# Attention's projections in a stage of their own, two blocks at once in seven products

## The chip, the cores and the metric

The kernel runs on one core of a Trainium2 chip. The core has a matrix engine (TensorE, PE in the profile, with its weight loads as PEld), VectorE (DVE), ScalarE (ACT), GpSimd (POOL), and SyncE (SP), which here issues most of the DMAs. Each engine works through its own queue in order; semaphores tie the queues together. The metric is the device time of one execution in microseconds; lower is better. PE is given its matrix products in a one-pass float32 format, so a float32 value is kept as two parts, a high and a low one, and a product is made of three matmuls.

## What is computed

A decoder trunk of two layers over 16 learned tokens and 1024 given ones, 1040 in all (L), with width 1024 and 16 heads of 64. Layer 0 is a state-space mixer and a gated feed-forward network, layer 1 attention and another such network. The change touches only what lies between the first network and the second: keys and values are projected from the normalized stream, queries from the same stream with another gain, and a "stick-breaking" attention follows.

```python
kv = _rmsnorm(h, kv_norm) @ w_kv
k_shared, v_shared = ...   # 16 heads of 64 each
q = (_rmsnorm(h, sb_norm[j]) @ sb_w_q[j]).reshape(b, L, SB_HEADS, SB_HEAD_DIM)
o = _stick_breaking_attention(q, k_shared, v_shared).reshape(b, L, SB_WIDTH)
h = h + o @ sb_w_o[j]
...
    logits = jnp.einsum('bthd,bshd->bhts', q[:, t0:t1], k[:, :t1]) * scale
    visible = s_idx < t_idx
    log_keep = jnp.where(visible, jax.nn.log_sigmoid(-logits), 0.0)
    later = lax.cumsum(log_keep, axis=3, reverse=True) - log_keep
    log_w = jnp.where(visible, jax.nn.log_sigmoid(logits) + later, -jnp.inf)
    w = jnp.exp(log_w)
    outs.append(jnp.einsum('bhts,bshd->bthd', w, v[:, :t1]))
```

The kernel writes a weight as a difference of two running products of keep probabilities, so the output of a head is a sum over differences of neighbouring values.

## The kernel before

Its stages follow one another: the mixer with its output projection, then the network's `up` and `down` products, attention, the projection of its output (`o_proj`), and `up` and `down` once more. Tokens lie along the columns and features along the 128 rows.

**The seven-product scheme.** `up` and `down` of layer 0 compute a 2 by 2 block product of matrices with seven products of half the size instead of eight (Strassen's scheme). `forms` and `up_sums` make the sums and differences of operands, and three of the products continue in PSUM banks that already hold others. In `up`, a product of a block is 4 x 3 matmuls of some 260 columns; `up` has 22 blocks on two token halves.

**What lies around attention.** `down` finishes in four column quarters of 260 tokens. Its last operation for a feature tile is the residual add in `accumulate` (line 399). After each of three token tiles (TT: 348, 348 and 344 columns) `to_attention` calls `norm`: it makes the high and low parts `uh`, `ul` of the stream, the square sums and the factor of the norm, and spills the stream to DRAM (`h1_d`).

**Attention.** It goes through eight pairs of heads. For each pair come 18 steps: a chunk i of 116 tokens (9 chunks) against a token tile jj of keys at or before it. In a step, `weigh` multiplies queries and keys of both heads (`lg`, 4 matmuls, line 1413), ACT makes the sigmoid (line 1414), POOL masks the diagonal chunk (`affine_select`, line 1418) and DVE scans the running products, once for each head (line 1422). `turn` transposes the result on PE (`wT`, up to 6, line 1435), and ACT copies it to SBUF (line 1439). When two chunks are complete, `values` multiplies them with the values (`po`, line 1450, in bursts of 12 to 60 matmuls), and ACT adds the value of the chunk's end as a bias (line 1457). The calls of this stage are made in an order written out by hand, and PE, DVE, ACT and POOL run in just that order: `flush(LAG)` with LAG = 2 puts the transposes of a step three steps behind its logits.

**The projections** lie between these steps. `heads` gives each pair a `load` of its weights (scaled on DVE, lines 1303 to 1307, split on ACT and DVE) and `half`, one half of a projection of one kind (k, q or v) for one token tile: 12 matmuls of 348 columns into a bank `pj`. The table `halves` of `attention` says which half falls in which step, most of them for the next pair. The results are scaled by the norm's factor on DVE, then `stack` (queries) and `key` (keys) bring high and low parts into the rows in which the products need them, with DMAs from SBUF to SBUF (lines 1356 to 1358 and 1373); `place` transposes the differences of the values (`pv`, line 1384). In the last pair, from its tenth step on, no projections remain, and the banks that they had go to the logits: four banks for `lg` instead of two.

The transfers of this stage are issued by SP in program order (178 of them), except for the outputs `o_d`, which ACT issues.

## Time and profile before

| what | before |
|---|---|
| median of 3 runs | 2854.01 us (2853.3 to 2854.32) |
| the profiled execution | 2852.52 us, span 2850.8 us, mean granted PE clock 0.997 |
| attention, from the last matmul of down to the first matmul of `o_proj` | 1526.15 to 2046.80 us, 520.65 us |
| one pair of heads | 64.50 us |

The profile lists busy time by engine, and beside it the trace gives groups of instructions by line, windows of time, the chain of work that ended last and the instructions in order. In a row of windows, the busy time of each engine stands with the number of instructions in parentheses, then the granted clock of PE as a share of the full one, the DMA engines' share and GB/s. In a row of groups, `x64 | 26.6, 424 | 17.1` means 64 instructions, 26.6 us busy, 424 ns each in the mean, and 17.1 us of idle time of the engine just before them. A busy time of PE counts each matmul from its start to its modelled end; these overlap, so what a matmul costs is read from the distance between starts.

### The profile page before, as it was taken

Reading aid. Unit: us, or ns where it says so; the run is one execution under the profiler, and the core shown is the slowest. Engines: PE = TensorE matmul, PEld = TensorE weight load, DVE = VectorE, ACT = ScalarE, POOL = GpSimd, SP = SyncE. Lnnn points to the kernel's source line nnn. Section 1 sums busy time; section 2 is a strip of 40 time slices with the busy share of each in tenths; the row PEclk is TensorE's granted clock in tenths of the full one; section 3 lists DMA queues with packets and bytes.
Section 4 is the critical chain, followed back from the end, with each engine's and each line's share of the span. In section 5 each row is a group of like instructions: output and inputs, shape, how many; then the busy total and the mean of one; then the engine's idle time right before and its main releaser. Section 6 shows DMA issues by size and latency. Waiting matters only on the chain.

```text
span 2850.8 us, 54962 instructions
## 1 busy us (share of the span) xinstructions
PE 2808.9 (99%) x21808; PEld 2698.9 (95%) x21808; DVE 2000.2 (70%) x3736; ACT 1551.8 (54%) x3060; POOL 619.2 (22%) x542
## 2 busy tenths in 40 slices
PE   8999999999999999999999999999999999999998
PEld 5999999999999999999999999999998999999888
DVE  5687777776587565658986666666679556557895
ACT  5578676673255555555334555555536555555442
POOL 0000000000005666650000111111002666661000
PEclk9999999999999999999999999999999999999999
DMA  6234333314322222236142222222441222225331
GB/s 178 68 111 118 101 103 96 108 58 165 97 80 75 82 76 81 77 102 205 53 136 82 68 67 62 71 62 55 153 145 55 82 76 81 82 76 185 111 111 60
DMA packets 134128, 274.69 MB, mean 96 GB/s; under 512 B 16464, under 2 KB 68304, under 8 KB 133872
## 3 DMA queue, kind: packets, MB, share of 16 engines
q1 hardware_dynamic: 128560, 260.26, 29.2%
q10 hardware_dynamic: 4048, 6.36, 0.6%
q0 software_dynamic: 1264, 4.57, 0.5%
q8 instruction: 171, 2.80, 0.4%
q14 instruction: 85, 0.70, 0.1%
HBM read 203.02 MB, written 53.21 MB: 90 GB/s over the span
## 4 chain that ended last, share of the span: by engine, by line
PE 87%; DVE 3%; DMA 1%; ACT 1%; issue 0%; ACTq 0%; DVEq 0%; SPq 0%
PE p L165 10%; PE p L167 10%; PE p L166 10%; PE acc L166 8%; PE acc L167 8%; PE acc L165 8%; PE pj L165 7%; PE pj L166 7%; PE pj L167 7%; PE lg L1413 3%; PE po L1450 3%; PE wT L1435 3%; PE y L679 1%; PE S L667 1%; PE y L681 1%; DVE bl L930 1%
## 5 line engine op out<-in xcount | busy, mean ns | idle before, releaser
L165 PE MATMUL pj<-uh,wh 128*128 128x348 f32 (+2 forms) x1536 | 500.7, 326 | 1.1 <-DVE h L399 1.1
L166 PE MATMUL pj<-ul,wh 128*128 128x348 f32 (+2 forms) x1536 | 495.1, 322 | 0.0
L167 PE MATMUL pj<-uh,wl 128*128 128x348 f32 (+2 forms) x1536 | 491.6, 320 | 0.0
L165 PE MATMUL p<-bh,fh 128*128 128x262 f32 (+1 forms) x1408 | 401.2, 286 | 10.4 <-DVE p L1054 4.9
L166 PE MATMUL p<-bl,fh 128*128 128x262 f32 (+1 forms) x1408 | 400.3, 285 | 0.5 <-DVE bl L930 0.2
L167 PE MATMUL p<-bh,fl 128*128 128x262 f32 (+1 forms) x1408 | 398.5, 284 | 0.3 <-DVE fl L985 0.3
L165 PE MATMUL p<-bh,wh 128*128 128x262 f32 (+1 forms) x1056 | 300.6, 285 | 1.0 <-ACT bh L929 1.0
L167 PE MATMUL p<-bh,wl 128*128 128x262 f32 (+1 forms) x1056 | 300.9, 285 | 0.0
L166 PE MATMUL p<-bl,wh 128*128 128x262 f32 (+1 forms) x1056 | 300.2, 284 | 0.6 <-DVE bl L930 0.6
L165 PEld LDWEIGHTS pj<-uh,wh 128*128 128x128 f32 x1536 | 288.5, 188 | 3.4 <-ACT wh L1313 1.3
L166 PEld LDWEIGHTS pj<-ul,wh 128*128 128x128 f32 x1536 | 289.0, 188 | 1.2
L167 PEld LDWEIGHTS pj<-uh,wl 128*128 128x128 f32 x1536 | 288.6, 188 | 0.1
L165 PEld LDWEIGHTS p<-bh,fh 128*128 128x128 f32 x1408 | 267.5, 190 | 12.4 <-DVE p L1054 5.3
L293 DVE SCALAR_TENSOR_TENSOR c<-p,params,c 128x260 f32<-128x260 f32 (+1 forms) x440 | 208.6, 482 | 92.7 <-ACT c L289 90.4
L166 PEld LDWEIGHTS p<-bl,fh 128*128 128x128 f32 x1408 | 267.8, 190 | 1.6 <-DVE bl L930 1.3
L167 PEld LDWEIGHTS p<-bh,fl 128*128 128x128 f32 x1408 | 266.7, 190 | 0.7 <-DVE fl L985 0.5
L985 POOL TENSOR_TENSOR fl<-x,fh 128x1024 fp32r<-128x1024 f32 x80 | 192.3, 2404 | 248.2 <-ACT fh L984 248.2
L1054 DVE TENSOR_TENSOR p<-p,ft 128x262 f32<-128x262 f32 (+1 forms) x176 | 76.5, 436 | 216.0 <-ACT ft L1051 124.0
L166 PE MATMUL acc<-gl,wh 128*128 128x260 f32 (+1 forms) x672 | 211.3, 320 | 0.4 <-DVE gl L1152 0.4
L167 PE MATMUL acc<-gh,wl 128*128 128x260 f32 (+1 forms) x672 | 208.7, 320 | 0.0
L165 PE MATMUL acc<-gh,wh 128*128 128x260 f32 (+1 forms) x672 | 204.0, 319 | 0.0
L165 PEld LDWEIGHTS p<-bh,wh 128*128 128x128 f32 x1056 | 201.1, 190 | 1.5 <-ACT bh L929 1.2
(320 smaller groups left out, 7223.9 us busy)
## 6 DMA issues: line engine op xcount, KB each, us to landing
w<-in_w_up SPq DMA_DIRECT2D x92, 512.0 KB
w<-in_w_down SPq DMA_DIRECT2D x44, 512.0 KB
w<-in_w_in SPq DMA_DIRECT2D x40, 512.0 KB
E<-ea_d SPq DMA_DIRECT2D x32, 464.0 KB
D<-acs_d SPq DMA_DIRECT2D x32, 420.5 KB
g<-c SPq DMA_DIRECT2D x88, 130.0 KB
g<-c SPq DMA_DIRECT2D x88, 128.0 KB
b<-g SPq DMA_DIRECT2D x16, 520.0 KB
```

What stands on the lines that cost most here:

```text
L165: mm(out, wh, uh, start=first, stop=False, skip_group_check=joins)
L166: mm(out, wh, ul, start=False, stop=False, skip_group_check=joins)
L167: mm(out, wl, uh, start=False, stop=last, skip_group_check=joins)
L293: nc.vector.scalar_tensor_tensor(to, ps[:, o + i : o + i + n], wcol(i), out, op0=ALU.mult, op1=ALU.add)
L667: nc.tensor.matmul(ps, bk[:n], xde[:n].rearrange("p h d -> p (h d)"), start=True, stop=True)
L679: nc.tensor.matmul(y, xdt[:n, i, :], dk[:, i, :], start=True, stop=c == 0)
L681: nc.tensor.matmul(y, state[:, i, :], ce[:, i, :], start=False, stop=True)
L985: (self.nc.vector if b < 2 else self.nc.gpsimd).tensor_tensor(lo[:, :n], t, hi[:, :n].bitcast(F32), op=ALU.subtract)
L1054: add = lambda o, x, y: tt(o[:, :N], x[:, :N], y[:, :N], op=ALU.add)
L1413: nc.tensor.matmul(ps[:nt, a, :m], part[:, c0 : c0 + nt], ks[a][:, s0 : s0 + m], start=x == 0, stop=x == 1)
L1435: nc.tensor.transpose(pt[:ns, x * CB : x * CB + nt], kp[a][:nt, x * CB : x * CB + ns], self.ident[:nt, :nt])
L1450: nc.tensor.matmul(po[64 * a : 64 * a + 64, w], v[: CH[c][1], c, 64 * a : 64 * a + 64], wt[a][: CH[c][1], c, :nt], start=x == 0, stop=x == ...
```

## The change

The projections leave attention and become a stage between `down` and attention, `head_rows`. It has 12 blocks (the list `HP`): queries, then values, then keys, each for four groups of two head pairs. Two neighbouring pairs and two neighbouring token quarters form the 2 by 2 scheme, so a block takes seven products of 4 x 3 matmuls with 260 columns for each of two token halves.

- `down` gets `end`: the residual add of its last quarter writes into tiles of its own instead of `h`. `head_entry` takes the place of `to_attention`: it spills the stream and makes the forms (`head_forms`) of the first token half while `down` runs. `norm`, `scaled_project` and the classes' `half`, `key`, `stack` and `place` are gone.
- The stream is not normalized before the products. `factors` reads it again from DRAM, makes the factor of the norm during the first blocks, and `put` multiplies keys and values by it; queries get it in the sigmoid's scale as before.
- `put` writes the results to DRAM: `q_d` (high and low part), `k_d` (four slabs of 64 rows) and `v_d`. `turned` reads the values again, makes the differences, transposes them and writes `vt_d`.
- `heads` has only loads left: keys, values and queries of a pair come from DRAM in the rows that the products need.
- In attention, `LAG` is 3 and `kp` has 8 buffers. `lg2` has two buffers throughout. The bias of the outputs is one add on DVE for two chunks, except where they lie in different token tiles; there ACT adds it as before. SP issues 514 transfers in the two stages, against 178 in the stage before.

```diff
-LAG = 2
+LAG = 3
+HP = [(k, p) for k in "qvk" for p in range(0, PAIRS, 2)]
...
-        self.nc.vector.tensor_tensor(h[f][:, o], h[f][:, o], ps[:, :n], op=ALU.add)
+        self.nc.vector.tensor_tensor(h[f][:, o] if to is None else to, h[f][:, o], ps[:, :n], op=ALU.add)
...
+    def head_forms(self, h, end, t, tiles, pool):
...
+        b12, b22 = ([end[k + x][:, :F] if t else h[k + x][:, c0 + F : c0 + 2 * F] for k in half] for x in (0, KD // 2))
...
+        yield from parts(0, b11, first)
+        yield from parts(1, b21)
+        yield from parts(5, b22, others)
+        yield from parts(2, b22, lambda k: tt(b22[k], b21[k], b22[k], op=ALU.subtract))
+        yield from parts(3, t1)
+        yield from parts(4, b12)
+        yield None
+        yield from parts(6, b22)
...
+        def put(kind, p, j, x):
+            x, c = x[:, :F], slice(F * j, F * j + F)
+            if kind == "q":
+                for i, y in enumerate(split(x)):
+                    nc.sync.dma_start(qd[p, i, :, c], y)
+                return
+            t = self.tmp(kind)[:, :F]
+            tt(t, x, r[:, HALO + F * j : HALO + F * j + F], op=ALU.mult)
+            if kind == "v":
+                nc.sync.dma_start(vd[p, :, c], t)
+                return
+            hi, lo = split(t)
+            for i in range(2):
+                nc.sync.dma_start(kd[p, 3 * i, :, c], hi[64 * i : 64 * i + 64])
+                nc.sync.dma_start(kd[p, 1 + i, :, c], lo[64 * i : 64 * i + 64])
...
+            x = product(0, self.mm("p"))
+            p1 = copy(x)
+            yield
+            y = product(2, self.sm("p"))
+            add(y, y, p1)
+            u2 = copy(y)
+            yield
+            z = product(3, (self.ex if next(turn) else self.lg)("p"))
+            p5 = copy(z)
+            add(z, z, u2)
+            yield
+            put(kind, p, 2 * t, product(1, x, False))
+            yield
+            add(p5, product(4, y, False), p5)
+            put(kind, p + 1, 2 * t + 1, p5)
+            yield
+            put(kind, p, 2 * t + 1, product(5, z, False))
+            yield
+            put(kind, p + 1, 2 * t, product(6, y, False))
...
+            for _ in zip(s, t):
+                for _ in range(4 if n < 4 else 2):
+                    next(chores, None)
...
+            if kind == "v":
+                chores = chain(chores, turned(p), turned(p + 1))
...
-        kp = pool.tile([P, 2, TW], F32, tag="kp", name=self.nm("kp"), bufs=6)
+        kp = pool.tile([P, 2, TW], F32, tag="kp", name=self.nm("kp"), bufs=8)
...
-            nc.scalar.activation(os[p][:, c0 : c0 + nt], po[:, b * CB : b * CB + nt], AF.Identity, bias=ends[:, i : i + 1])
...
+            nc.vector.tensor_tensor(three(os[i0 // 3 * 3][:, c0 : c0 + k * nt], nt), three(po[:, : k * nt], nt),
+                                    ends[:, i0 : i1 + 1].unsqueeze(2).to_broadcast([P, k, nt]), op=ALU.add)
...
+        loads = {(0, 2): ("q", 2), (-1, 9): ("k",), (-1, 10): ("q", 0), (-1, 11): ("v",), (-1, 13): ("q", 1)}
...
-                ps = both(more if p + 1 == PAIRS and n > 8 and n % 2 else self.lp)
+                ps = self.lp.tile([P, 2, 512], F32, tag="lg2", name=self.nm("lg"), bufs=2)
...
-                for own, pair in now.items():
-                    if (own, n) in halves:
-                        late += pair.half(*halves[own, n])
```

PE's queue in the middle of a pair, before the change: transposes `wT`, logits `lg`, and then the first of 12 matmuls of a projection (`pj`, from the stream's parts `uh`, `ul` and the weights' parts `wh`, `wl`).

```order
L1435 MATMUL wT_21715<-ident,kp_21573 116x116 x3
L1435 MATMUL wT_21720<-ident,kp_21573 116x116 x3
L1413 MATMUL lg_21725<-k_21142,qs_21499 116x116 x2
L1413 MATMUL lg_21725<-k_21143,qs_21501 116x116 x2
L165 MATMUL pj_21737<-uh_16937,wh_21458 128x348
L166 MATMUL pj_21737<-ul_16938,wh_21458 128x348
L167 MATMUL pj_21737<-uh_16937,wl_21459 128x348
```

The same queue after the change, in a pair's later steps:

```order
L1573 MATMUL lg_21580<-k_21354,qs_21409 116x348 x2
L1573 MATMUL lg_21580<-k_21355,qs_21412 116x348 x2
L1595 MATMUL wT_21595<-ident,kp_21467 116x116 x3
L1595 MATMUL wT_21600<-ident,kp_21467 116x116 x3
L1573 MATMUL lg_21605<-k_21354,qs_21409 116x348 x2
L1573 MATMUL lg_21605<-k_21355,qs_21412 116x348 x2
L1595 MATMUL wT_21619<-ident,kp_21497 116x116 x3
L1595 MATMUL wT_21624<-ident,kp_21497 116x116 x3
```

Logits and transposes now follow one another with nothing between them, except for the bursts of `po`.

DVE's queue at the end of `down`, before the change: the last residual add (line 399), then the low parts of the first pair's weights, their scaling, and the low part and squares of the last token tile.

```order
L399 TENSOR_TENSOR h_14628<-h_14628,acc_17369 128x260
L1315 TENSOR_TENSOR wl_17457<-w_2276_17450,wh_17456 128x512
L1307 TENSOR_TENSOR w_2281_17462<-w_2281_17462,params 128x512 x2
L270 TENSOR_TENSOR ul_16952<-h_14628,uh_16951 128x344
L237 TENSOR_TENSOR sq_17405<-sq_17405,sq_17425 128x344
```

After the change, from the 22nd row behind the last residual add: low parts of a form (line 1279), scaling of the next block's weights (1313), the first two adds between products of the first block (1468), and further forms (1289).

```order
L1279 TENSOR_TENSOR bl_17478<-ft_17354,bh_17477 128x260
L1313 TENSOR_TENSOR w_2313_17752<-w_2313_17752,params 128x512
L1468 TENSOR_TENSOR p_17455<-p_17455,c_17431 128x260
L1289 TENSOR_TENSOR ft_17291<-ft_17291,ft_17437 128x260
L1313 TENSOR_TENSOR w_2383_18141<-w_2383_18141,params 128x512
L1289 TENSOR_TENSOR ft_17312<-ft_17312,ft_17441 128x260
L1313 TENSOR_TENSOR w_2383_18141<-w_2383_18141,params 128x512
L1289 TENSOR_TENSOR ft_17333<-ft_17333,ft_17445 128x260
L1289 TENSOR_TENSOR ft_17354<-ft_17354,ft_17449 128x260
L1468 TENSOR_TENSOR p_17487<-p_17487,c_17469 128x260
```

The first of these adds is the 28th row behind the last residual add, the second the 35th.

SP's queue in a block of keys after the change, with stores of four half tiles and of turned values:

```order
L1404 DMA k_d<-hi_20444 64x260
L1405 DMA k_d<-lo_20445 64x260
L1404 DMA k_d<-hi_20444 64x260
L1405 DMA k_d<-lo_20445 64x260
L1449 DMA vt_d<-vt_20461 116x2x128
L1449 DMA vt_d<-vt_20464 116x128
```

Before the change SP had no stores to DRAM here besides those of the stream.

More of the change, by code (lines that the diff above doesn't have):

```diff
@@ L1090, in up, with down @@
         return d
-    def down(self, layer, gd, hd, pool, after):
+    def down(self, layer, gd, hd, pool, after, end=None):
         nc, a, F = self.nc, self.a, FNS[layer]
@@ new lines, in head_entry @@
+    def head_entry(self, h, j, res, h1, end, pool):
+        F = FNS[0]
+        if res is None:
+            forms = [{}, {}]
+            res = [self.head_forms(h, end, t, forms[t], pool) for t in range(2)], forms, []
+        works, forms, first = res
+        if j == 0:
+            self.spill_tile(h, h1, 0, 2 * F)
+            for _ in range(6 * KD // 2):
+                next(works[0])
+        elif j == 1:
+            self.spill_tile(h, h1, 2 * F, F)
+            g, v = self.head_raw(0)
+            first += [g, v, *self.head_sums(0, g, v, pool)]
+        else:
+            for k in range(KD):
+                self.nc.sync.dma_start(h1[k, :, 3 * F :], end[k][:, :F])
+            for _ in works[0]:
+                pass
+        return res
@@ new lines, in turned, with block, product, copy @@
+                yield
+        def block(n, t, w):
+            kind, p = HP[n]
+            def product(i, ps, start=True):
+                wh, wl, c0 = w[i]
+                for k in range(KD // 2):
+                    c = slice(c0 + k * P, c0 + k * P + P)
+                    self.mm3(ps[:, :F], wh[:, c], wl[:, c], *forms[t][i][k], start and k == 0, k == KD // 2 - 1, not start)
+                return ps
+            def copy(ps):
+                s = self.ft(pool) if n else self.tmp("c")
+                nc.scalar.activation(s[:, :F], ps[:, :F], AF.Copy)
+                return s
+            add = lambda o, x, y: tt(o[:, :F], x[:, :F], y[:, :F], op=ALU.add)
+            x = product(0, self.mm("p"))
+            p1 = copy(x)
+            yield
+            y = product(2, self.sm("p"))
+            add(y, y, p1)
+            u2 = copy(y)
+            yield
+            z = product(3, (self.ex if next(turn) else self.lg)("p"))
+            p5 = copy(z)
+            add(z, z, u2)
+            yield
+            put(kind, p, 2 * t, product(1, x, False))
+            yield
+            add(p5, product(4, y, False), p5)
+            put(kind, p + 1, 2 * t + 1, p5)
+            yield
+            put(kind, p, 2 * t + 1, product(5, z, False))
+            yield
+            put(kind, p + 1, 2 * t, product(6, y, False))
+            yield
@@ new lines, in head_rows @@
+        turn = cycle((0, 0, 1))
+        rest, chores = works[1], iter(())
+        for n, (kind, p) in enumerate(HP):
+            if n == 0:
+                w = self.head_weights(0, *first, pool)
+            else:
+                g, v = self.head_raw(n)
+                w = self.head_weights(n, g, v, *self.head_sums(n, g, v, pool), pool)
+            s, t = (block(n, t, w) for t in range(2))
+            if n == 0:
+                for _ in s:
+                    for _ in range(5):
+                        next(rest, None)
+                for _ in rest:
+                    pass
+                for _ in t:
+                    pass
+                chores = factors()
+                continue
+            for _ in zip(s, t):
+                for _ in range(4 if n < 4 else 2):
+                    next(chores, None)
+            if n == 3:
+                for _ in chores:
+                    pass
+            if kind == "v":
+                chores = chain(chores, turned(p), turned(p + 1))
@@ L1392, in token_factors @@
+        for _ in chores:
+            pass
+        return qd, kd, vt
+    def token_factors(self, r):
         nc = self.nc
[L1393 removed]
         for j, (s0, _) in enumerate(TT):
@@ L1488, in flush @@
                     ready.append((p, i))
[L1490 to L1500 removed]
+        for x in (("k",), ("q", 0), ("v",), ("q", 1)):
+            pairs[0].load(*x)
         for p in range(PAIRS):
```

318 lines of the change are left out of this document (162 added, 156 removed).

## Prediction

> **What bounds the kernel now.** I first read the busy times and the chain that ended last:
>
> ```profile
> PE 2808.9 (99%) x21808; PEld 2698.9 (95%) x21808; DVE 2000.2 (70%) x3736; ACT 1551.8 (54%) x3060; POOL 619.2 (22%) x542
> PE 87%; DVE 3%; DMA 1%; ACT 1%; issue 0%; ACTq 0%; DVEq 0%; SPq 0%
> ```
>
> TensorE (PE) is busy for 99% of the span and carries 87% of the chain, so the time is what PE has to do plus the few places where it waits. The view by windows, cut at the attention stage and at one whole pair inside it, comes next (columns: window, its length, then the busy time and count of each engine, the granted clock, the DMA share and GB/s):
>
> ```profile
> 1526.15:2046.80 520.65, 518.94 (x4551) 500.39 (x4549) 342.01 (x544) 294.26 (x682) 58.76 (x168) 1.00 0.26 72
> 1692.76:1757.26 64.50, 64.50 (x569) 62.38 (x571) 41.98 (x67) 36.14 (x84) 7.21 (x21) 1.00 0.23 63
> ```
>
> The stage takes 520.65 us and PE idles for less than 2 of them. A pair takes 64.50 us, all PE; VectorE (DVE) is busy 41.98 and ScalarE (ACT) 36.14, so each has over 20 us of slack. That slack comes from the projections: while PE multiplies them, the others catch up with sigmoids, scans and copies. The same windows for the tile `pj`, the projections alone (a stretch of 48 back to back, then the stage; PE, PEld, DVE and ACT):
>
> ```profile
> 1527.55:1535.17 7.62, 7.62 (x48) 7.49 (x48) 0.52 (x1) 0.00 (x0) 1.00 0.52 165
> 1526.15:2046.80 520.65, 297.45 (x1728) 274.87 (x1728) 48.79 (x96) 21.58 (x48) 1.00 0.26 72
> ```
>
> Busy times of matmuls overlap (they are pipelined), so the 297.45 are not time taken. One projection matmul advances PE by 7.62/48 = 0.1588 us; 1728 of them take 274.4 us.
>
> **The change part by part.** All sums are made against the profiled execution, 2852.52 us, whose span is 2850.8. It lies 1.5 us under the median of the runs, 2854.01, and the predicted time is on its footing.
>
> *The products.* They leave attention (-274.4) and come back as 12 blocks x 2 token halves x 7 products x 4 x 3 = 2016 matmuls of 260 columns. The trace has this shape of work in both up stages, with 262 and with 258 columns:
>
> ```profile
> 950.00:1000.00 50.00, 50.00 (x415) 50.00 (x414) 27.63 (x60) 26.37 (x54) 32.16 (x20) 1.00 0.25 83
> 2300.00:2350.00 50.00, 50.00 (x418) 50.00 (x418) 30.75 (x68) 28.09 (x56) 34.46 (x21) 1.00 0.23 77
> ```
>
> 50/415 and 50/418 give 0.1205 and 0.1196; for 260 columns I take 0.1200, so 2016 x 0.1200 = 241.9 us. Difference: **-32.5**. The transposes of the values, 9 for a pair, are moved from attention to the new stage: nothing.
>
> *The start of the stage.* The first projection waited for the last residual add of down:
>
> ```profile
> 1526.15 0.28 PE L167 MATMUL acc<-g,wl 128*128 128x260 f32 x1
> 1527.55 0.40 PE L165 MATMUL pj<-uh,wh 128*128 128x348 f32 x1 [1.12 <-DVE h L399]
> ```
>
> The first block's operands come from the first token half, made during down, so this wait goes: **-1.1**. Late next are the combinations in that block. In the changed order 27 rows of DVE stand between the last add of down and the add that the fifth product waits for: forms of the second half and the scaling of the next weights. Rows of before for such operations:
>
> ```profile
> L399 DVE TENSOR_TENSOR h<-h,acc 128x260 f32<-128x260 f32 x64 | 26.6, 424 | 17.1 <-PE acc L167 16.8
> L930 DVE TENSOR_TENSOR bl<-ft,bh 128x262 fp32r<-128x262 f32 x32 | 13.8, 485 | 0.0
> L1307 DVE TENSOR_TENSOR w<-w,params 128x512 f32<-128x512 f32 x48 | 31.0, 685 | 0.1
> ```
>
> At 0.42 to 0.69 us a row, 27 rows take 11 to 18 us if nothing overlaps, while the four products ahead give PE 48 x 0.12 = 5.8 us. So PE stalls here by several us. The nearest stretches that hold such a start are the entries of up:
>
> ```profile
> 850.00:900.00 50.00, 45.97 (x357) 44.06 (x358) 40.64 (x92) 31.00 (x67) 23.84 (x15) 1.00 0.20 65
> 2150.00:2200.00 50.00, 43.06 (x302) 41.17 (x301) 47.68 (x116) 30.90 (x71) 11.35 (x7) 0.90 0.11 36
> ```
>
> PE lost 50 - 45.97 = 4.0 us in one and 6.9 in the other. I take their mean, **+5.5**; bounds 0 (all of it done during down) and 12 (18 less the 5.8). The second entry also ran at a granted clock of 0.90, the first at 1.00. [...]
>
> *The rest of the new stage.* Its DVE, ACT and POOL work is like that of up, where PE had no idle time in 50 us, with DVE at 27.63. New are the ways through DRAM. Each k block issues 32 stores of 64 rows, 2 loads of weights and some 11 transfers of the turned values on SP, in that order. SP's own rows for such issues:
>
> ```profile
> 1706.30 0.33 SPq L1296 DMA_DIRECT2D w<-in_w_q  x1
> 1709.84 0.47 SPq L1356 DMA_DIRECT2D k<-k  x1
> 1712.20 0.59 SPq L1358 DMA_DIRECT2D k<-klo  x1
> ```
>
> At 0.47 to 0.59 and 0.33 this is 32 x 0.47 + 13 x 0.33 = 19.3 to 23.2 us of SP for a block of 168 x 0.12 = 20.2 us of PE. Behind a late store wait the buffer it reads (8 of a kind), then the DVE and ACT operation that writes it, then the PSUM bank, then PE; behind it on SP wait the next weights and the reads of v_d. Bounds: 0 as in up, and 4 x 3 = 12 for the four k blocks at the end plus some 6 for transposes that find their values late, 18. As the q and v blocks issue far less, and PE in up never waited, I take the lower part: **+4**.
>
> *The start of attention.* The bank pools change hands, and for the first four steps there is neither a transpose nor a projection between the logits. Its loads stand ahead of the last stores of k on SP, so they don't wait for the stage's end. Before, the first pair's projections filled this time. Bounds 0 and 6 (four steps of logits and sigmoids, about 1.4 each, below); I take **+2.5**.
>
> *Attention without projections.* This term decides. What is left for PE in a pair is 64.50 - 216 x 0.1588 = 30.2 us, 29.2 without the transposes of values (three in 0.33 us, nine in 1.0, by the chain below). Against it stand the other engines in the same window, by line: scans on DVE, sigmoids on ACT, copies of transposes on ACT, then POOL's masks.
>
> ```profile
> 1692.76:1757.26 64.50, 26.55 (x37) 1.00 0.23 63
> ...
> 1692.76:1757.26 64.50, 13.49 (x18) 1.00 0.23 63
> ...
> 1692.76:1757.26 64.50, 12.94 (x38) 1.00 0.23 63
> ...
> 1692.76:1757.26 64.50, 4.21 (x9) 1.00 0.23 63
> ```
>
> DVE 26.6 plus four adds of 0.42 (the bias, moved from ACT) is 28.2, ACT 26.4: three engines near 29 us, in lockstep. The end of the last pair already runs so, with no projections, and with four banks for logits. Its timeline:
>
> ```profile
> 2032.34 0.87 PE L1413 MATMUL lg<-k,qs 128*116 128x348 f32 x4
> 2033.04 1.10 PE L1435 MATMUL wT<-ident,kp 116*116 116x116 f32 x6
> 2033.62 0.84 ACT L1414 ACTIVATE kp<-lg,rt 116x696 f32<-116x696 f32 x1
> 2033.91 0.87 PE L1413 MATMUL lg<-k,qs 128*116 128x348 f32 x4
> 2035.03 0.88 ACT L1414 ACTIVATE kp<-lg,rt 116x696 f32<-116x696 f32 x1
> 2035.15 0.86 PE L1413 MATMUL lg<-k,qs 128*112 128x344 f32 x4
> 2036.48 0.87 PE L1413 MATMUL lg<-k,qs 128*112 128x348 f32 x4
> 2037.91 0.87 PE L1413 MATMUL lg<-k,qs 128*112 128x348 f32 x4
> ```
>
> Sigmoids follow each other by 1.41 us. An unhindered step of PE is 0.60 + 0.64 = 1.24 by the chain of a pair with projections:
>
> ```profile
> 1731.52 0.64 PE lg L1413 x4
> ...
> 1734.05 0.60 PE wT L1435 x6
> ...
> 1736.96 3.13 PE po L1450 x60
> ...
> 1741.24 0.33 PE pv L1384 x3
> ```
>
> From 2033.91 to 2037.91 three steps took 4.00 instead of 3.72: 0.093 lost in each. The step from 2032.34, right behind a burst of `po` in which ACT had run dry, took 1.57: 0.33 lost. A pair has 12 full steps and 5 bursts, so 12 x 0.093 + 5 x 0.33 = 2.8 us. Another way agrees: ACT's 26.4 can't run during the bursts (9.98 us of PE in this window by the line of `po`, L1450) but for one sigmoid of 0.85 in each, 26.4 + 9.98 - 4.25 = 32.1 us for a pair instead of 29.2. For seven and a half pairs (the last half ran so before): 7.5 x 2.8 = **+21**. The row by which the 9.98 stands:
>
> ```profile
> 1692.76:1757.26 64.50, 9.98 (x182) 8.87 (x184) 1.00 0.23 63
> ```
>
> Bounds: 0 if the lag of three steps covers everything, and 7.5 x (26.4 + 9.98 - 29.2) = 54 if nothing of ACT lies beside a burst.
>
> Sum: -32.5 - 1.1 + 5.5 + 4 + 2.5 + 21 = -0.6, so **2851.9 us**: the saved products are paid back by lost cover.
>
> **The rivals.**
>
> *The longer lag covers the bursts.* A transpose now comes four steps behind its logits instead of three, and POOL, DVE and ACT keep a store of work for the bursts; then only 12 x 0.093 x 7.5 = 8.4 are left of the 21: -13.2, 2839.3 us. For it: the adds leave ACT. Against it: in the trace it was ACT, working on the step's own sigmoid and the copies of an older one, that set the pace, and a lag doesn't shorten ACT's work.
>
> *ACT paces attention altogether.* If no sigmoid lies beside a burst, a pair takes 36.4 and the term is 54: 2884.9 us. For it: two banks for logits now, where the last pair had four, so a sigmoid that is late holds the logits two steps on. Against it: in the rows above a sigmoid did start while PE was at work. It decides once a full step takes over 1.41. The Trainium skill, "Perfetto Trace Analysis", section "Optimization Strategy", states that kernels with several regimes may gain by interleaving them; this change takes apart what was interleaved, and by that rule it would lose. The pair's 64.50 us of PE without an idle one agree with the rule for the kernel before.
>
> *SP's order stalls the k blocks: the other side.* If a 64-row store costs SP more than (20.2 - 13 x 0.33)/32 = 0.50 us in the mean, SP needs longer than PE for a k block; at 0.59 it is 3 us in each of four, +12 on top of the 4: 2863.9 us, slower. For it: rows of 0.47 and 0.59 on both sides of the point. Against it: eight buffers, and lighter blocks ahead that leave SP in advance.
>
> **How the numbers follow.** Forecast (2842 to 2862) 0.45, the lag covers 0.27, SP's order 0.18, ACT paces 0.10. A measurement of this kernel can tell about 0.2%, 5.7 us, from no change. The forecast's 0.45 is 0.13 faster, 0.20 same, 0.12 slower; the lag's 0.27 is faster but for 0.02; of SP's, 0.06 is same and 0.02 faster (with a cheap attention); ACT's is slower. Faster 0.40, same 0.28, slower 0.32. The range runs from 2832 (lag covers, entry at its 4.0, nothing for the rest) to 2866 (SP's order, and 2 more): outside lie ACT's 0.10 and as much of the other tails.
>
> **What would show it.** In the profile after: matmuls of the new stage at 0.120 each over about 255 us; an idle PE in the first block, ended by DVE; in the k blocks idle time ended by a DMA (SP's order) or none; in attention a pair's period between two `po` of 12: 32 us by the forecast, 30.2 by the lag, 36 by ACT, with PE's idle time ended by ACT copies or sigmoids. I am wrong if that period is under 30 or above 34, or if the new stage is longer than 265.

## The result and the profile after

The changed kernel takes 2967.78 us (median of 4 runs, 2965.53 to 2973.33) against 2853.66 us before: a ratio of 1.0403, 95% interval 1.0385 to 1.0421. It is slower by 114 us, where the prediction had no change and a range up to 2866. The profiled execution is the longest of the four, 2973.33 us with a span of 2971.6, so 120.8 us over the span before; the terms below are made against these two spans.

The page of the changed kernel, busy times and chain:

```profile
PE 2827.1 (95%) x22098; PEld 2696.7 (91%) x22098; DVE 2081.1 (70%) x3883; ACT 1568.0 (53%) x3128; POOL 790.4 (27%) x616
...
PE 25%; issue 10%; DVE 2%; DMA 1%; ACT 1%; POOL 0%; SPq 0%; POOLq 0%; ACTq 0%; DVEq 0%
```

PE fell from 99% to 95% of a longer span: it is idle for 144.5 us (2971.6 - 2827.1), where it was for 41.9 before. The chain can no longer be followed along PE. The windows say where. The rows are, in order: the first block of queries, the other three, the values, the keys, then the first pair of attention, a pair in its middle and the last one (columns as before):

```profile
1525.30:1566.60 41.30, 25.24 (x172) 23.39 (x171) 32.89 (x67) 18.97 (x50) 24.95 (x11) 0.83 0.21 68
1566.60:1654.80 88.20, 73.05 (x524) 70.65 (x523) 62.99 (x106) 40.40 (x96) 45.53 (x25) 0.88 0.53 163
1654.80:1741.10 86.30, 84.31 (x701) 83.74 (x700) 48.60 (x84) 29.29 (x61) 64.21 (x65) 1.00 0.46 142
1741.10:1874.95 133.85, 95.63 (x717) 93.23 (x715) 61.63 (x109) 39.39 (x96) 52.07 (x69) 0.86 0.51 136
1874.95:1923.20 48.25, 34.66 (x226) 30.34 (x226) 27.97 (x44) 23.73 (x53) 4.60 (x12) 0.68 0.66 172
1956.80:1990.60 33.80, 31.10 (x346) 27.40 (x343) 26.90 (x41) 23.87 (x59) 5.60 (x9) 1.00 0.51 128
2125.70:2168.30 42.60, 39.45 (x466) 34.54 (x464) 31.86 (x48) 29.43 (x74) 5.61 (x9) 1.00 0.33 113
```

A block is 168 matmuls, 20.2 us at the predicted 0.120. The four blocks of values run close to that (86.3 us for 80.6, with transposes of values among them), at a clock of 1.00. The first block takes twice its time, the next three 88.2 for 60.5, the keys 133.9 for 80.6, all with a clock of 0.83 to 0.88. A pair of attention takes 33.80 and the first one 48.25. So the saving in products is there, and everything around it costs more than was summed.

### The profile page after: what moved, and what is told of

Read it like the earlier page. It is cut to its first block, busy times and chain, and to the rows that moved or that the text cites. A ratio compares the mean times of both kernels' runs of the same rounds, so it can differ in the third digit from the quotient of the medians.

```text
span 2971.6 us, 56854 instructions
## 1 busy us (share of the span) xinstructions
PE 2827.1 (95%) x22098; PEld 2696.7 (91%) x22098; DVE 2081.1 (70%) x3883; ACT 1568.0 (53%) x3128; POOL 790.4 (27%) x616
## 3 DMA queue, kind: packets, MB, share of 16 engines
q1 hardware_dynamic: 181232, 309.28, 33.7%
## 5 line engine op out<-in xcount | busy, mean ns | idle before, releaser
L166 PE MATMUL p<-bh,fh 128*128 128x262 f32 (+2 forms) x1792 | 518.2, 290 | 30.6 <-ACT c L1465 11.7
L167 PE MATMUL p<-bl,fh 128*128 128x262 f32 (+2 forms) x1792 | 515.9, 288 | 0.4 <-DVE bl L907 0.2
L168 PE MATMUL p<-bh,fl 128*128 128x262 f32 (+2 forms) x1792 | 512.7, 288 | 0.3 <-DVE fl L962 0.3
L166 PE MATMUL p<-bh,wh 128*128 128x262 f32 (+2 forms) x1344 | 382.8, 285 | 7.8 <-DVE lo L1388 4.4
L167 PE MATMUL p<-bl,wh 128*128 128x262 f32 (+2 forms) x1344 | 381.8, 284 | 0.7 <-DVE bl L907 0.5
L168 PE MATMUL p<-bh,wl 128*128 128x262 f32 (+2 forms) x1344 | 381.6, 284 | 0.7 <-DVE wl L1339 0.7
L166 PE MATMUL pj<-uh,wh 128*128 128x348 f32 (+2 forms) x960 | 313.8, 327 | 0.0
L167 PE MATMUL pj<-ul,wh 128*128 128x348 f32 (+2 forms) x960 | 310.7, 324 | 0.0
L167 PEld LDWEIGHTS p<-bl,wh 128*128 128x128 f32 x1344 | 254.9, 190 | 2.0 <-DVE bl L907 1.4
L168 PEld LDWEIGHTS p<-bh,wl 128*128 128x128 f32 x1344 | 254.6, 190 | 1.0 <-DVE wl L1339 0.9
```

What stands on the lines that cost most here:

```text
L166: mm(out, wh, uh, start=first, stop=False, skip_group_check=joins)
L167: mm(out, wh, ul, start=False, stop=False, skip_group_check=joins)
L168: mm(out, wl, uh, start=False, stop=last, skip_group_check=joins)
```

## What PE waits for

**In the new stage.** The view of waits for PE between 1525 and 1875 us (who waited for what: us in total, times, the longest):

```profile
PE pv L1443 <- DVE dv L1437: 34.8, 11, 11.7
PE p L166 <- ACT c L1465: 12.0, 3, 9.2
PE p L166 <- ACT ft L1465: 5.0, 5, 3.7
PE p L166 <- DVE lo L1388: 4.4, 2, 2.7
```

About half of PE's idle time there is the transposes of values, which wait for the difference `dv`, which waits for the read of `v_d`. SP's own timeline in the middle of the key blocks shows why that read is late:

```profile
1806.94 0.46 SPq L1404 DMA_DIRECT2D k_d<-hi  x1
1807.49 0.55 SPq L1405 DMA_DIRECT2D k_d<-lo  x1
1808.09 0.59 SPq L1404 DMA_DIRECT2D k_d<-hi  x1
1808.73 0.59 SPq L1405 DMA_DIRECT2D k_d<-lo  x1
...
1818.16 0.54 SPq L1430 DMA_DIRECT2D v<-v_d  x1
...
1819.28 0.38 SPq L1433 DMA_DIRECT2D v<-v_d  x1
```

SP issues a store about every 0.6 us, without a pause, over 11 us; the reads that PE waits for stand behind 16 stores of k and two of turned values. Over the same time PE stands for 11.7 us. Once the read is out (1818.16), the next `dv` starts 2.5 us later: what is late is the issue, not the transfer.

**At its start**, the timeline of POOL, SP, DVE and PE:

```profile
1527.18 10.03 POOL L1339 TENSOR_TENSOR fl<-x,fh 128x1024 fp32r<-128x1024 f32 x1 [251.28 <-ACT fh L1338]
...
1533.90 1.11 DVE L1279 TENSOR_TENSOR bl<-ft,bh 128x260 fp32r<-128x260 f32 x3
...
1538.46 0.81 SPq L1309 DMA_DIRECT2D w<-in_w_q  x2
...
1542.09 0.69 DVE L1313 TENSOR_TENSOR w<-w,params 128x512 f32<-128x512 f32 x1 [7.07 <-DMA w<-in_w_q]
...
1544.54 0.58 PE L166 MATMUL p<-bh,fh 128*128 128x260 f32 x1 [9.22 <-ACT c L1465]
```

One subtraction on POOL takes 10.03 us, where the same shape takes 2.4 in `up`. It starts while DVE works row after row, and ends 2.2 us after DVE's last one (1535.0). The low part of the weights stands behind it on POOL, and SP waits for that before it loads the next weights:

```profile
SPq L1309 <- POOL wl L1339: 11.7, 1, 11.7
```

So these come only from 1538 on, DVE stands 7.07 us for them, and the add of the first block is queued behind. The Trainium skill, "SBUF — State Buffer", section "SBUF: two separate sides", says that DVE and GpSimd share one pair of ports as an exclusive lock; this row and its time fit that, and so do rows of k_rows (below), though no run here shows the ports themselves.

**In attention**, at a burst of `po` (2015.33), the timeline of PE, ACT and DVE:

```profile
2015.33 2.40 PE L1610 MATMUL po<-wt,v 116*64 116x116 f32 x44
2015.59 0.93 ACT L1574 ACTIVATE kp<-lg,params 116x696 f32<-116x696 f32 x1
2017.20 1.75 DVE L1582 TENSOR_TENSOR_SCAN kp<-kp,kp,one 116x348 f32<-116x348 f32 x2
2018.87 0.37 DVE L1619 TENSOR_TENSOR o<-po,params 128x232 f32<-128x232 f32 x1
2019.32 0.33 ACTq L1628 DMA_DIRECT2D o_d<-o  x1
2019.75 0.43 ACT L1599 ACTIVATE wt<-wT 116x116 f32<-116x116 f32 x2 [3.23 <-DVE o L1619]
```

The burst ends at 2017.7, but the add of the bias on DVE stands behind two scans and runs at 2018.87. ACT issues the store of that output, in its own queue, and waits there until 2019.32; its copies of transposes come behind, 3.23 us idle, and PE's next transposes behind those.

## The experiments

The table has the times (of one run each, but for after, together and three), the new stage from down's last matmul to the first logits, the blocks 1 to 3 of queries, the last three blocks of keys, and the first and a middle pair of attention. Starts of instructions in the traces give the stretches.

| kernel | us | new stage | blocks 1-3 | last three k | first pair | middle pair |
|---|---|---|---|---|---|---|
| after | 2967.8 | 349.7 | 88.2 | 110.9 | 48.2 | 33.8 |
| k_rows | 2933.8 | 322.7 | 83.2 | 90.7 | 36.0 | 33.7 |
| factors_slow | 2965.1 | 341.2 | 83.5 | 105.8 | 48.1 | 33.8 |
| turn_first | 2962.9 | 343.4 | 85.4 | 110.5 | 48.1 | 33.4 |
| start_dve | 2960.7 | 337.6 | 85.7 | 106.2 | 49.2 | 33.8 |
| apart | 2932.0 | 318.0 | 87.7 | 80.2 | 39.2 | 33.7 |
| apart_early | 2939.8 | 320.5 | 87.5 | 76.6 | 43.9 | 33.7 |
| no_factors | 2916.0 | 301.3 | 62.0 | 90.0 | 36.8 | 33.7 |
| no_mask | 2965.2 | 349.2 | 85.3 | 110.2 | 48.1 | 32.7 |
| act_plus | 2989.1 | 345.8 | 86.2 | 109.1 | 48.6 | 36.4 |
| dve_plus | 2994.7 | 347.0 | 85.4 | 109.7 | 48.6 | 37.4 |
| vt_act | 2956.4 | 342.8 | 86.4 | 101.4 | 38.0 | 33.7 |
| together (4 runs) | 2951.2 | 316.9 | 80.2 | 82.8 | 44.0 | 36.8 |
| bare_before | 2624.4 | | | | | 31.5 |
| bare_after | 2968.5 | 349.9 | 85.3 | 110.7 | 43.4 | 33.7 |
| lag4 | 2978.7 | 353.1 | 88.8 | 110.4 | 46.7 | 33.8 |
| ends_dve | 2945.2 | 332.2 | 84.3 | 95.5 | 36.1 | 33.8 |
| bias_act | 2951.6 | 341.8 | 85.0 | 108.8 | 46.7 | 31.9 |
| three (4 runs) | 2930.5 | 323.8 | 86.7 | 91.3 | 39.0 | 32.0 |

In the eight of these whose new stage has the code of `after` (turn_first, no_mask, act_plus, dve_plus, bare_after, lag4, bias_act and it itself), the stage took 341.8 to 353.1, its first block 37.9 to 44.7, blocks 1 to 3 85.0 to 88.8 and the last three of keys 108.8 to 110.9. A difference in one run is read against that spread (the first block is counted from its first matmul here).

### Stores of k: k_rows

```diff
-            hi, lo = split(t)
-            for i in range(2):
-                nc.sync.dma_start(kd[p, 3 * i, :, c], hi[64 * i : 64 * i + 64])
-                nc.sync.dma_start(kd[p, 1 + i, :, c], lo[64 * i : 64 * i + 64])
+            for i, y in enumerate(split(t)):
+                nc.sync.dma_start(kd[p, i, :, c], y)
```

> The high and the low part of a key tile go to DRAM in one store of 128 rows each, instead of two of 64: 64 stores less on SP, 16 loads more. Theory 'SP is late': in the k blocks SP issues one store each 0.64 us without a pause, so 64 fewer free about 41 us of it; the waits of PE's transposes for the values (35 us) and of the buffers shrink, the new stage (1525 to 1875 us) gets 30 to 45 us shorter, and the first pair of attention falls from 48 to under 40 us. Rival 'two steps are too short': the read of v_d and its use lie two products apart, too near for a transfer through DRAM whatever SP does; then the stage changes by less than 10 us.

The windows of k_rows: blocks 1 to 3, all four blocks of keys and the first pair of attention:

```profile
1564.80:1648.00 83.20, 69.98 (x524) 68.14 (x523) 60.65 (x105) 40.77 (x96) 47.47 (x27) 0.94 0.57 173
...
1734.40:1847.60 113.20, 91.11 (x716) 88.98 (x715) 58.63 (x108) 39.36 (x95) 53.08 (x68) 0.93 0.62 173
1847.60:1883.60 36.00, 27.84 (x225) 24.43 (x226) 25.90 (x42) 22.99 (x53) 5.80 (x12) 0.78 0.73 191
```

34 us less in all, the new stage 27 less (somewhat under what the theory had), the last three key blocks 110.9 to 90.7, the first pair 48.2 to 36.0. It is far outside the spread, and the clock rose with it from 0.86 to 0.93. PE's waits for the values in the new stage, 34.8 us before this edit, are down to

```profile
PE pv L1441 <- DVE dv L1435: 18.5, 9, 8.8
```

So SP's late issue costs some 20 us in these blocks, and the rival falls. 30 us over the matmuls' 60.5 remain.

### What is left in the blocks of keys: apart, apart_early, vt_act, ends_dve

All four stand on k_rows. apart:

```diff
-            hi, lo = (self.tmp(s)[:, :F] for s in ("hi", "lo"))
+            hi, lo = (self.ft(pool)[:, :F] for s in ("hi", "lo"))
...
-            t = self.tmp(kind)[:, :F]
+            t = self.ft(pool)[:, :F]
```

> On top of k_rows: the scaled tile and its two parts in put come from the ring of twelve ft tiles, so the ring of eight U tiles is left to the values on their way through v_d. Theory 'shared ring': a read of v_d waits on SP for a buffer that an earlier store of k holds, and everything behind it on SP waits too; apart, the last three k blocks (91 us in k_rows for 61 us of matmuls) get 10 to 25 us shorter. Rival 'two steps are too short': one step of 2.9 us between read and use is less than issue and landing take in any case; then they stay within 5 us.

80.2 instead of 90.7 in these blocks, at the low end of the theory, but the first pair took 39.2 and blocks 1 to 3 87.7, so the time is the same. Buffers count for some of the wait, and it comes back elsewhere.

apart_early reads all three tiles of a pair ahead of the first use:

```diff
+            ts = []
             for j, (s0, n) in enumerate(TT):
...
+                ts.append(t)
                 yield
                 yield
+            for j, (s0, n) in enumerate(TT):
+                t = ts[j]
```

> As apart, and each pair's three reads of v_d are issued three steps (some 8.6 us) ahead of their use instead of one. Theory 'shared ring': like apart, within 5 us. Rival 'two steps are too short': the last three k blocks get 15 to 25 us shorter than in apart, PE's waits for dv nearly vanish and with them the lower clock.

Only 3.6 less than apart there, and the first pair rose to 43.9: 7.8 us slower than apart in all. Two steps were not too short by themselves; in the form in which it was put, this theory falls. The three reads of a pair also hold three buffers of the ring at once, which this run doesn't separate.

vt_act:

```diff
-                    nc.sync.dma_start(vt[p, 3 * j + x : 3 * j + y, :m].rearrange("c t d -> t c d"), o)
+                    nc.scalar.dma_start(vt[p, 3 * j + x : 3 * j + y, :m].rearrange("c t d -> t c d"), o)
```

> On top of k_rows: the 48 stores of turned values are issued by ACT, right behind the copies that make them, instead of by SP. Theory 'SP waits in order': in k_rows SP stood up to 6 us at a store of turned values whose copy was not made yet, with stores of k and reads of v_d behind it; off SP, the last three k blocks (91 us in k_rows) get 8 to 18 us shorter and the first pair of attention (36) loses 1 to 3. Rival 'latency of the way through v_d': the reads come no earlier, and the k blocks stay within 5 us.

The opposite: 101.4 instead of 90.7, and 22.6 us slower than k_rows. The theory falls. In the trace the wait moved: in the last three blocks of keys SP stood 8.1 us for the high parts that ACT makes in k_rows, and here 38.6. ACT itself issued 22 stores in its queue there, 7.6 us in all; how that grew to 30 us more stays open.

ends_dve:

```diff
-                    nc.gpsimd.tensor_copy(self.ends[:, 9 * p + 3 * j + i : 9 * p + 3 * j + i + 1], t[:, last : last + 1])
+                    nc.vector.tensor_copy(self.ends[:, 9 * p + 3 * j + i : 9 * p + 3 * j + i + 1], t[:, last : last + 1])
```

> On top of k_rows: the copies of the chunks' last values (72 of one column) are made on DVE instead of POOL. Theory 'POOL's queue': on POOL they wait for the reads of v_d (36 us in the k blocks), and behind them wait the sums and low parts of the next block's weights; without it the last three k blocks (91 us in k_rows) get 8 to 20 us shorter. Rival 'values on their way': PE's transposes and the buffers wait for v_d as before, and the k blocks stay within 5 us.

95.5, not shorter: POOL's queue isn't it. What holds the values on their way in the remaining 30 us stays open after these four.

### Blocks 1 to 3: factors_slow, no_factors

```diff
-                for _ in range(4 if n < 4 else 2):
+                for _ in range(2):
```

> The chores of the norm's factors (32 reads of the stream, squares, sums) are spread over the blocks 2 to 4 with two a step instead of four. Theory 'burst of reads': the idle time of PE between 1545 and 1645 us (about 25 us with the lower clock behind it) comes from reads that stand in SP's queue among the stores of q, and from a ring of eight buffers shared with them; spread out, this part gets 8 to 20 us shorter. Rival 'DVE and POOL slow each other': rows of DVE beside POOL's take 2 to 4 times their usual time there; then the part stays within 5 us.

83.5 against 85.0 to 88.8: at most a few us, under what the theory had and inside the rival's 5. Spreading the same work helps little.

no_factors, on k_rows and start_dve:

```diff
-                chores = factors()
+                chores = iter(())
```

> On top of k_rows and start_dve: leaves out the norm's factors of attention (the reads of the stream, squares, sums and roots); the factor is set to 1. Theory 'factors fill the q blocks': blocks 1 to 3 (83 us in k_rows for 60.5 us of matmuls) take 60 to 69 us, so the new stage is 14 to 23 us shorter there. Rival 'DVE beside POOL': the weights' sums on POOL and DVE hold each other up and that stays; the three blocks take over 76 us.

The window of blocks 1 to 3 without the factors:

```profile
1567.30:1629.30 62.00, 62.00 (x506) 62.00 (x505) 32.90 (x58) 26.60 (x55) 43.39 (x25) 0.97 0.50 156
```

62.0 us, PE without an idle one and DVE down from 60.65 in k_rows to 32.90, though POOL worked on (43.39 after 47.47). So the factors cost 21 us in these blocks, and the rival as it was put, that the weights' sums alone hold PE up, falls. By which queue they cost it isn't separated, and a slower DVE can be part of it: its subtractions with both operands in SBUF (`lo<-ft,hi`) took 1.92 us in the mean of five in k_rows, and 0.71 in the mean of six without the factors. Four of the five began while POOL was at work and ended 0.3 us behind POOL's row, two of them here:

```profile
1615.19 1.49 POOL L1323 TENSOR_TENSOR x<-x,w 128x512 f32<-128x512 f32 x1
1615.44 1.52 DVE L1388 TENSOR_TENSOR lo<-ft,hi 128x260 fp32r<-128x260 f32 x1
...
1618.05 2.57 POOL L1339 TENSOR_TENSOR fl<-x,fh 128x1024 fp32r<-128x1024 f32 x1
1618.30 2.61 DVE L1388 TENSOR_TENSOR lo<-ft,hi 128x260 fp32r<-128x260 f32 x1
```

### The first block: start_dve

```diff
-        e = [nc.gpsimd] * 4 if n else [nc.vector] * 2 + [nc.gpsimd] * 2
+        e = [nc.gpsimd] * 4 if n else [nc.vector] * 4
```

> The low parts of the first block's weights are all made on DVE; POOL makes none. Theory 'POOL beside a busy DVE': one subtraction on POOL took 10.03 us (2.4 elsewhere) while DVE was busy; it held a weight buffer, the load of the next weights and so DVE, which stood 7 us for that load ahead of the add that PE wanted. Without it the wait of 9.2 us at 1544 goes, and 5 to 9 us are saved with the clock behind it. Rival 'DVE's rows': the rows between set the wait, and with two more of 1.3 us it stays or grows by 1 to 3.

The single wait of 9.2 us went, into several of 0.7 to 4.1 us. The block took 36.3 us against 37.9 to 44.7, and 36.6 in `three`, but 39.1 in no_factors, which has the edit too. A gain of some 2 to 5 us, not settled by these runs. POOL's first subtraction was still stretched (8.45 us). The cause of the single wait is shown with it, its price only roughly.

### Attention: turn_first, no_mask, act_plus, dve_plus

turn_first:

```diff
+            full = list(ready) if ready and (ready[-1][1] % 2 or ready[-1][1] == 8) else []
             if len(turns) > n:
...
+            if full:
+                p = full[0][0]
+                self.values(p, [(i, wts.pop((p, i))) for _, i in full], pairs[p].v, pairs[p].ends, os, od)
+                del ready[: len(full)]
```

> In attention a step's transposes now stand ahead of the burst of po on PE instead of behind it; nothing else is changed. Theory 'ACT runs dry in the bursts': copies of transposes can then lie beside the burst, and a pair takes 30 to 32 us instead of 33.8, 15 to 30 us less in all. Rival 'DVE paces': scans of 26.6 us and adds with their waits for POOL set 33.8, and a pair stays within 0.7 of it.

33.4: inside the rival's 0.7. That ACT runs dry in the bursts is not what sets the pair.

no_mask, on turn_first:

```diff
-            nc.gpsimd.affine_select(out=own, in_=own, ...)
```

> On top of turn_first: leaves out the mask of the diagonal chunks on POOL. Theory 'the mask stands in DVE's way': DVE waits about 5 us in a pair for POOL's masks, ahead of scans that could run, and is the pacemaker with 27 us of its own; without them a pair takes 28.5 to 31.5 us instead of 33.4. Rival 'ACT paces': sigmoids and copies, 1.41 us for a full step, and idle time in the bursts of po set the period; it stays above 32.7.

32.7, just where the rival's bound was drawn: the masks cost 0.65 us of a pair, not 2 or more.

act_plus and dve_plus add one operation to each step:

```diff
+        more = pool.tile([P, 256], F32, tag="more", name=self.nm("more"), bufs=1)
+        nc.scalar.activation(more, self.params[:, :256], AF.Copy)
```

> The changed kernel with one more copy of 128x256 on ACT behind each sigmoid, into a tile that nothing reads: 18 in a pair. Theory 'ACT paces attention': most of its cost is seen, a pair grows from 33.8 by two thirds or more of 18 times its time (about 0.3 us each by the rows of this size), so by 3.5 us or more, to over 37.3. Rival 'the path through DVE paces': it is hidden in ACT's idle time for the most part, and a pair grows by less than 2 us.

```diff
+        more = pool.tile([P, 256], F32, tag="more", name=self.nm("more"), bufs=1)
+        nc.vector.tensor_tensor(more, self.params[:, :256], self.params[:, 256:512], op=ALU.add)
```

> The changed kernel with one more add of 128x256 on DVE ahead of each step's scans, into a tile that nothing reads: 18 in a pair, some 0.33 us each. Theory 'ACT paces attention': DVE's 27 us of 33.8 hide much of it, and a pair grows by less than 3 us. Rival 'the path through DVE paces': a pair grows by 4 us or more.

The added operations alone, in the window of one pair, act_plus first and dve_plus behind:

```profile
2014.00:2050.40 36.40, 8.30 (x18) 1.00 0.46 119
```

```profile
2014.00:2051.30 37.30, 7.30 (x18) 0.95 0.47 116
```

8.30 us on ACT lengthened the pair by 2.6, 7.30 us on DVE by 3.6, of which a part is the clock (0.95 in that pair): each between the two theories. Neither engine paces alone, and "ACT paces" falls in the form in which it was put.

### Whose price is it: bare_before, bare_after, lag4, bias_act

```diff
-        pairs = [self.heads(u, p, pool) for p in range(PAIRS)]
+        pairs = [self.heads(u, 0, pool)] * PAIRS
...
-                    if (own, n) in halves:
+                    if p == 0 and (own, n) in halves:
```

> The kernel before with the first pair's queries, keys and values used for all eight pairs: the projections of the other seven are left out, their work on DVE, ACT and SP too; from the second pair on the logits have four banks as after the change. Theory 'cover': attention without projections costs what the changed kernel shows, 33 to 35 us for a pair, whatever stage the projections went to. Rival 'the changed attention is slow by its own doing' (lag, loads from DRAM, adds on DVE): the pair falls to 29 to 31.5 us, what PE has to do.

bare_after does the same to the changed kernel, with its table `loads`:

> The changed kernel with the first pair's queries, keys and values used for all eight pairs: attention's loads from DRAM are left out from the second pair on. Theory 'cover': a pair stays at 33.8 within 0.5. Rival 'loads': it falls by 1 us or more.

The window of one pair of bare_before:

```profile
1654.20:1685.70 31.50, 31.05 (x344) 27.84 (x343) 26.02 (x37) 25.66 (x67) 5.72 (x9) 1.00 0.06 19
```

The attention of before, bared of its projections, takes 31.5 us a pair, the upper end of the rival's range; the changed one without its loads takes 33.7. So 2.3 us of the 4.6 over PE's own 29.2 are the price of the lost cover, and as much is the changed attention's own doing. The loads account for 0.1 of it.

lag4:

```diff
-LAG = 3
+LAG = 4
```

> The changed kernel with a lag of four steps instead of three. Theory 'a ring of engines in order' (logits, sigmoid, mask, scan, transposes, copies; act_plus and dve_plus each saw about half of what was added): another step of store lets each engine run on past the others' waits, and a pair falls by 0.7 to 2 us. Rival 'the work between two bursts is the bound': the lag doesn't matter, within 0.4.

33.8: a longer lag doesn't help.

bias_act:

```diff
-        if i0 // 3 == i1 // 3:
+        if i0 > i1:
...
-            for b, i in enumerate((i0, i1)):
+            for b, i in enumerate(range(i0, i1 + 1)):
```

> The changed kernel with the bias of the outputs added on ACT for every chunk, as before the change; the lag stays at three. Theory 'the bias in DVE's queue': its add on DVE waits for the burst of po to end, and the scans of the next steps stand behind it; back on ACT a pair takes 31.2 to 32.2 us, as in bare_before, some 12 to 16 us less in all. Rival 'the lag': three steps instead of two set the 33.7 and the bias doesn't matter; a pair stays above 33.2.

```profile
1945.50:1977.40 31.90, 31.03 (x345) 27.39 (x343) 25.83 (x37) 25.65 (x66) 5.61 (x9) 1.00 0.55 138
```

31.9, with ACT's busy time up from 23.87 to 25.65 and PE's idle time down from 2.7 to 0.9 us. The bias in DVE's queue cost 1.9 us a pair; the rival, the lag, falls. The path isn't the one that was expected (scans behind an add that waits for the burst): DVE has no wait for `po` in the changed kernel's five pairs from 1956.8 on. There ACT waits for the add, at the store of the output, as in the timeline above:

```profile
ACT wt L1599 <- DVE o L1619: 23.3, 8, 3.3
```

In bias_act this row is gone, and ACT waits for the burst itself (25.3 us in five pairs).

### Several at once: together, three

together holds k_rows, start_dve, factors_slow, apart, turn_first and vt_act; three holds k_rows, start_dve and bias_act.

> k_rows, start_dve, factors_slow, apart, turn_first and the stores of turned values on ACT in one kernel. If the causes are separate, their gains add: 40 + 5 to 10 + 5 + 5 + 5 + about 10, so 2895 to 2905 us, still slower than before by some 45, since the factors (21 us) and attention without cover (33.4 for a pair) remain. If they are one cause seen in several places, it stays above 2915.

2951.2 us, ratio to before 1.0341 (1.0324 to 1.0359): not the sum. It holds vt_act, which loses by itself, and its pairs took 35 to 37.5, which no part of it alone shows. In two of these pairs the clock was 0.95 (1.00 in turn_first), and between 1930 and 2080 the transposes' weight loads waited up to 3.8 us at a time for ACT's copies (0.8 there); why the copies came late stays open.

> k_rows, bias_act and start_dve in one kernel. If the three causes are separate, the gains add: 2968 less 34 (k_rows), about 14 (the pairs of bias_act, 1.8 in each) and 5 (the first block of start_dve): 2910 to 2920 us, pairs at 32 us, first block at 36 us, the last three k blocks at 91. If they hang together, a pair stays above 33 or the k blocks grow by over 8, and the time is above 2925.

2930.5 us, ratio 1.0268 (1.0251 to 1.0285), the shortest of the versions that compute all, though not told apart from apart's single 2932.0. The middle pairs are at 31.9 to 32.1, except two of 33.8 and 34.8, the keys where k_rows had them and the first block at 36.6; the time is 10 us over the upper end of what adding gave. The stretches named kept their gains, two pairs apart, but the time is over the 2925 that were set as the sign that the three hang together: blocks 1 to 3 and the first pair took 6.5 us more than in k_rows (86.7 for 83.2, 39.0 for 36.0), and why isn't shown. No version found here beats the kernel before.

## Why the prediction was wrong

Against the 520.65 us of the stage before stand 643.0 (1525.3 to 2168.3). Point by point:

- **The products** (-32.5): right. In the blocks of values, at full clock, PE does 701 instructions in 86.3 us, transposes included; the products save what was summed.
- **The wait at the stage's start** (-1.1): gone, as said. **The first block** (+5.5, bounds 0 and 12): measured 41.3 - 20.2 = 21.1. The step counted 27 rows of DVE and let them run; it left out that one of them, the scaling of the next weights, needs a load, that the load needs a buffer that POOL must free, and that POOL, beside a busy DVE, took 10 us for 2.4. The mechanism was a queue on DVE, but with a wait in it.
- **The rest of the new stage** (+4, bounds 0 and 18): this is the step that failed most. (The profile was to show the step wrong by a new stage over 265 us; it took 349.7.) Blocks 1 to 3 cost 27.7 over their matmuls, the values 5.7, the keys 53.3: 86.7, of which some 8 are the transposes of values that came from attention (72 at 0.11). The prediction had SP's rate and the point from which it decides, 0.50 us a store, but summed it as 3 us a block of issue time. The stores run at about 0.6, and a late SP doesn't cost its own excess: reads that PE's transposes need stand behind the stores, and each such wait was up to 11.7 us. k_rows shows it, with 20 us in the keys. The factors were priced at nothing, "like up", and cost 21 (no_factors). The rival on SP's order named a cause and had 12 for it. What holds the keys for the other 30 us isn't shown.
- **The clock.** The prediction read it at the entries of up (0.90 beside 1.00) and put nothing for it into the sum. In the new stage, the 1985 distances under 0.45 us between starts of neighbouring matmuls add up to 261.0 us, where 0.12 each make 238.2: 22.8 us, and 19.9 without the 12 distances that hold a short wait. So some 20 us of the loss are a slower clock, and the windows with idle time are those at 0.83 to 0.88, the values almost without it at 1.00. Two neighbouring windows show how it comes:

```profile
1605.28:1608.69 3.41, 0.91 (x7) 0.91 (x8) 3.41 (x12) 1.53 (x5) 0.00 (x0) 1.00 0.81 254
1608.69:1612.10 3.41, 3.41 (x16) 3.21 (x15) 1.75 (x5) 1.55 (x4) 0.00 (x0) 0.50 0.97 235
```

PE is idle for 2.5 us of the first, and the second runs at half the clock. The Trainium skill, "TensorE: Matmul & The Clock Gate", section "HAM oscillation", warns of idle gaps over about 3.4 us. Here shorter ones were enough: the longest wait in that first window was 2.70 us, and in the second entry of up before the change, at 0.90, no wait was over 2.78. So the gaps cost a second time: some 20 us of slow matmuls on 71.4 us of idle time in this stage.
- **The start of attention** (+2.5): measured 48.2 - 33.8 = 14.4, at a clock of 0.68. The prediction had the loads ahead of the last stores in SP's order. Nine of the pair's twelve reads of queries stood there; three stood behind the last store and were issued at 1894.66, 20 us after its first logits, and the logits waited 4.0 us for them. In k_rows all twelve came ahead, and the pair took 12 us less.
- **Attention without projections** (+21): the price of the lost cover was about right: 29.2 + 2.8 = 32.0 for a pair was worked out from the last pair of before, and bare_before took 31.5, bias_act 31.9. That ACT running dry in the bursts makes this price isn't shown: with the transposes ahead of the burst a pair gained only 0.4 us (turn_first). The changed kernel took 33.8, since the bias on DVE was read as a relief of ACT ("the adds leave ACT"), while ACT's queue had to wait for it. With the first pair taken out, attention lost 41.7 instead of 21 (293.3 less 14.4 and less 237.2; these are an estimate of what the stage before had beside its projections: 520.65 - 1.1 - 274.4 and 8 for the transposes of values).
- Two of the rivals failed with it. The lag of three didn't cover the bursts, nor did one of four (lag4), and "ACT paces attention" was not it; that rival also said "two banks for logits now", which is wrong: `lg2` has two buffers of two banks each, so four.

The sum as measured: -32.5 - 1.1 + 21.1 + 86.7 - 8 + 14.4 + 41.7 = 122.3 us. It meets the difference of the two stretches (643.0 - 520.65 = 122.35) by the way it is made, since the 237.2 were taken from the stage before.

How far could the change go? Twelve blocks at 20.2 with 8 for the transposes are 250, and the attention of bias_act, with its first pair like the others, is 279.8 - (46.7 - 31.9) = 265. That makes 515, an estimate, against 520.65. By it, even with all of the new stage's waits gone, some 5 us would be won: of the 33.6 that the products and the first wait save, attention without its projections takes most back.

## What to carry to other kernels

Work that fills the gaps between dependent engines has a value of its own, which can be read where the kernel already runs without it (here its last pair); take it into the sum before moving the work out. When a change adds transfers to a queue that works in order, don't price the queue's own excess time: look for the first read that a busy engine needs and count what stands ahead of it. And an operation that is moved to relieve an engine must not leave behind, in that engine's queue, an instruction that waits for it.

## What the runs showed of the hardware

- A store of 64 rows by 260 columns took SP 0.45 to 0.60 us in a row of such stores, one of 128 rows mostly 0.32 to 0.55 in k_rows. Half as many stores of the same bytes made the keys' blocks 20 us shorter.
- A subtraction of 128x1024 on POOL took 10.03 us beside a DVE without pauses, 2.40 in the mean of 80 in `up`. DVE's rows can be the stretched ones too: in blocks 1 to 3 of k_rows its subtractions with both operands in SBUF took 1.92 us (five), those with one in PSUM 0.42 (17). Four of the five ended 0.3 us behind the row of POOL in which they began.
- Idle time was followed by a lower clock: 0.50 in the 3.41 us behind a wait of 2.70, 0.83 to 0.88 over blocks in which PE was idle for 17 to 39%, 0.68 in the first pair of attention, some 20 us of longer matmuls in one stage.
